# The opening of a hybrid Fourier/Hyena and attention block: loads, filters, modulation and norm in an order written out by hand

## The chip, the cores and the metric

The kernel runs on one core of one Trainium2 chip. The metric is the device time of one execution in microseconds (us). Work in a core is done by engines that run side by side, each with its own list of instructions: PE (matrix products), DVE (VectorE), ACT (ScalarE), POOL (GpSimd) and SP, which here issues the transfers from memory (DMA). An instruction waits on semaphores for what it needs from another engine.

## The reference

The block has two layers over 512 tokens and 256 context tokens of width 1024, in float32. Layer 0 has the mixer with which this case deals; layer 1 has latent attention; each layer ends in a gated feed-forward network (FFN) with a short convolution. Cut to the opening of layer 0:

```python
mod = silu(cond) @ w_mod + b_mod            # six parts: shift, scale, gate, twice
h = rms_norm(x) * (1 + scale) + shift       # for x and for the context
proj = h @ w_in                             # 1024 -> 4*128 (Fourier) + 3*512 (Hyena)
y_f = fft2(proj[..., :512]).real            # in four groups of 128
x0, x1, v = split(dwconv3(proj[..., 512:]), 3)

h_ = sin(f * (z @ w1 + b1)); h_ = sin(f * (h_ @ w2 + b2)); h_ = sin(f * (h_ @ w3 + b3))
h_ = (h_ @ w4) * decay                      # a filter in time, forward and backward halves
two_sided = concat(h_fwd, 0, reversed h_bwd)
spectrum = rfft(two_sided / sum(abs(two_sided)))
y_h = x0 * (irfft(rfft(v * x1) * spectrum) + v * x1 * bias)
out = concat(y_f, y_h) @ w_out
```

The filter and its spectrum are needed twice: for length 512 and for the context's length 256.

## The kernel before

**Precision.** Every product that counts is made of three matmuls: an operand is split into a high part (`hi`, L97, on ACT) and a low part (`lo`, L102, on DVE), and `mm3` (L116 to L118) adds high x high, high x low and low x high. A table or weight tile of 128 x 1024 (name `wr`) is loaded by SP (`wload`) and split in the same way into `wh` and `wl`; the normalized input has the parts `hh` and `hl`.

**The opening.** It has these parts, and the tile framework's scheduler orders the instructions of each engine from the order in the source, what depends on what, and its estimates of costs.

- The filter MLP (`filter_mlp`, `sine`): three rounds of a matmul (L330), eight DVE operations (L305 to L314) and a sine on ACT (L315).
- The time filters (`filter_time`), in six tiles of 128 positions: tiles 4 and 5 for the context, 0 to 3 for x. For each: two matmuls for 128 x 1024 results (L345), two products with the decay on DVE (L351, L352), their sum and difference on POOL (L357), which are split into high and low parts (`aph`, `apl`, `amh`, `aml`), two absolute values on ACT and their sum on POOL (L366). The sums of all tiles go through PE (L371) and a reciprocal on DVE (L373), which gives S.
- The spectra (`filter_spec`): two for the context and four for x, each a table times the filter tiles, then scaled with S (L403 to L405); `brow` is the bias in all partitions, which L381 rescales for each length; the Nyquist row comes from L389 to L392.
- The modulation: `gemv_pe` makes the shift and the scale of the first norm, in four chunks of 2 MB (`wm`): 16 matmuls with a 32-column operand, a copy on ACT (L182), small matmuls (L185) and an add on DVE (L190). The other parts come later and in pieces of 128 rows (`gemv_dve`), with a DVE product of the weight tile and the activated condition `sb` (L200). `make_A` turns scale and norm weight into the factor A.
- The norm (`norm`), for x (512 columns) and context (256): `stat` squares on ACT (L223) and sums on PE (L224); `fin` copies (L228), brings the sums into columns (`rt`, L232), takes 1/sqrt by Newton steps on DVE (`rsqrt`), and spreads it over the partitions (R, L238); `apply` multiplies on DVE (L248), adds the shift on ACT (L250, which gives `hh`) and takes the rest on DVE (L251, `hl`). There are eight tiles for x and eight for the context, so 32 DVE operations.

**The projections.** Sixteen tiles of w_in, 48 matmuls each, in the order 12, 8, 13, 9, 14, 10, 15, 11 (pairs v and x1), 4, 5, 6, 7 (x0), 0 to 3 (Uf). A projection of the Hyena part is convolved on the way out of PSUM (L294 on ACT, L295 and L296 on DVE); of a pair, POOL multiplies (L489, L490), DVE folds the halves (L494, L495), and PE transposes the result (`turn`, L501). The source puts a turn behind the next projection:

```python
hconv(12 + i, cv)
if folded:
    turn(i - 1, folded.pop())
hconv(8 + i, cx)
folded.append(fold(i, cv, cx))
...
hconv(4, x0[0])
turn(3, folded.pop())
```

A projection also issues one `gemv_dve`. The 32 tiles of layer 0's rest are spread over the 16 projections and, two per step, over the last steps of W_out (`res_proj` with `hook`); those of layer 1 go three to each step of the first FFN (`fill`).

Of the kernel before, what the change touches and what calls it, by code (L numbers as in the profile page):

```python
# [18 lines left out]
P = 128  # L19
D = 1024  # L20
KD = 8
# [29 lines left out]
class Builder:  # L51
# [10 lines left out]
    def pool(self, name, bufs=1, space=None, side=None):  # L62
        st = ExitStack()
        kw = {}
        if space is not None:
            kw["space"] = space
        if side is not None:
            kw["side"] = side
        p = st.enter_context(self.tc.tile_pool(name=name, bufs=bufs, **kw))
        self.stacks = getattr(self, "stacks", {})  # L70
        self.stacks[name] = st
        return p
# [31 lines left out]
    def wload(self, src, n=1024):  # L104

        raw = self.t(self.W, [P, 1024], F32, "wr")
        self.nc.sync.dma_start(raw[:, :n], src)
        h = self.t(self.W, [P, 1024], F32R, "wh")
        l = self.t(self.W, [P, 1024], F32R, "wl")
        self.hi(h[:, :n], raw[:, :n])  # L110
        self.lo(l[:, :n], raw[:, :n], h[:, :n])
        return h, l
# [57 lines left out]
    def gemv_pe(self, i, chunk):  # L170
# [3 lines left out]
        raw = self.t(self.wm, [P, 4096], F32, "wm")  # L174
        for half in range(2):
            nc.sync.dma_start(raw[:, 2048 * half : 2048 * half + 2048], self.I["wmod0a"][chunk, :, 2048 * half : 2048 * half + 2048])
# [34 lines left out]
    def norm(self, i, k, x, hh, hl, c0, n, tp):  # L211
# [33 lines left out]
        def apply(d):  # L245
            A, B = self.A[i][k][:, j, :], self.mod[i][:, 24 * k : 24 * k + 8, j]
            u = tp()
            nc.vector.scalar_tensor_tensor(u[:, :n], x[d][:, c0 : c0 + n], A[:, d : d + 1], box["R"][:, :n], op0=ALU.mult, op1=ALU.mult)  # L248
            dst = hh[d][:, c0 : c0 + n]
            nc.scalar.activation(dst, u[:, :n], AF.Identity, bias=B[:, d : d + 1])  # L250
            nc.vector.scalar_tensor_tensor(hl[d][:, c0 : c0 + n], u[:, :n], B[:, d : d + 1], dst.bitcast(F32), op0=ALU.add, op1=ALU.subtract)  # L251

# [64 lines left out]
    def filter_mlp(self):  # L317
        nc, I = self.nc, self.I
        p = self.pf
        zT = self.t(p, [66, 384], F32, "zT")  # L320
        fw = self.t(p, [P, 3, P], F32, "fw")
        w4 = self.t(p, [P, 1024], F32, "w4")
        nc.sync.dma_start(zT, I["zT"])
        nc.sync.dma_start(fw, I["fw"])
        nc.sync.dma_start(w4, I["w4"])
        h = zT
        for l in range(3):
            ps = self.ms()
            K = 66 if l == 0 else P
            nc.tensor.matmul(ps[:, :384], fw[:K, l, :], h[:K, :384], start=True, stop=True)  # L330
            h = self.t(self.S2, [P, 512], F32, "s2")
            self.sine(ps, self.col(f"fb{l + 1}"), h)
        return h, w4

    def filter_time(self, h3, w4, tts, nhalf):

        nc, I = self.nc, self.I
        v = nc.vector
        sums = []
        ap, am = [], []  # L340
        for i, tt in enumerate(tts):
            ps = self.mm()
            r0, c = 64 * (tt // 3), 128 * (tt % 3)
            for q in range(2):
                nc.tensor.matmul(ps[:, 512 * q : 512 * q + 512], h3[r0 : r0 + 64, c : c + 128], w4[r0 : r0 + 64, 512 * q : 512 * q + 512],  # L345
                                 start=True, stop=True)
            dec = self.t(self.S2, [P, 512], F32, "s2")
            nc.sync.dma_start(dec, I["decay"][tt])
            f = self.t(self.S2, [P, 512], F32, "s2")
            b = self.t(self.S2, [P, 512], F32, "s2")  # L350
            v.tensor_tensor(f, ps[:, 0:512], dec, op=ALU.mult)  # L351
            v.tensor_tensor(b, ps[:, 512:1024], dec, op=ALU.mult)  # L352
            if i == 0:
                v.memset(b[0:1, :], 0.0)
            for lst, op in ((ap, ALU.add), (am, ALU.subtract)):
                s = self.t(self.S2, [P, 512], F32, "s2")
                nc.gpsimd.tensor_tensor(s, f, b, op=op)  # L357
                tg = "ap" if lst is ap else "am"
                hi = self.t(p_ := self.pf, [P, 512], F32R, tg + "h", 4)
                lo = self.t(p_, [P, 512], F32R, tg + "l", 4)  # L360
                self.hi(hi, s)
                self.lo(lo, s, hi)
                lst.append((hi, lo))
            nc.scalar.activation(f, f, AF.Abs)
            nc.scalar.activation(b, b, AF.Abs)
            nc.gpsimd.tensor_tensor(f, f, b, op=ALU.add)  # L366
            sums.append(f)
        ps = self.ms()
        on = self.onesN[nhalf]
        for i, f in enumerate(sums):  # L370
            nc.tensor.matmul(ps, on, f, start=i == 0, stop=i == len(sums) - 1)  # L371
        S = self.t(self.pf, [P, 512], F32, "S")
        v.reciprocal(S, ps)  # L373
        return ap, am, S

    def filter_spec(self, ap, am, S, nhalf, fts, tt0):

        nc, I = self.nc, self.I
        v = nc.vector
        B = self.brow  # L380
        nc.vector.tensor_scalar(B, B, self.bscale / nhalf, None, op0=ALU.mult)  # L381
        self.bscale = nhalf
        nt = len(ap)
        ny = None
        if 0 in fts:
            ps = self.ms()
            for i in range(nt):
                for q in range(2):
                    nc.tensor.matmul(ps[0:1, :], self.altr, ap[i][q], start=i == 0 and q == 0, stop=i == nt - 1 and q == 1)  # L389
            ny = self.t(self.S2, [P, 512], F32, "s2")  # L390
            v.tensor_tensor(ny[0:1, :], ps[0:1, :], S[0:1, :], op=ALU.mult)
            v.tensor_tensor(ny[0:1, :], ny[0:1, :], B[0:1, :], op=ALU.add)  # L392
        H = []
        for ft in fts:
            th, tl = self.wload(I["ftab"][ft, :, 0 : 256 * nt], 256 * nt)
            ps = self.mm()
            for c, a in ((0, ap), (1, am)):
                for i in range(nt):
                    w = slice(256 * i + 128 * c, 256 * i + 128 * c + 128)
                    self.mm3(ps[:, 512 * c : 512 * c + 512], th[:, w], tl[:, w], a[i][0], a[i][1], i == 0, i == nt - 1)  # L400
            hr = self.t(self.S2, [P, 512], F32, "s2")
            hi = self.t(self.S2, [P, 512], F32, "s2")
            v.tensor_tensor(hr, ps[:, 0:512], S, op=ALU.mult)  # L403
            nc.gpsimd.tensor_tensor(hr, hr, B, op=ALU.add)
            v.tensor_tensor(hi, ps[:, 512:1024], S, op=ALU.mult)  # L405
            H.append((hr, hi))
        return H, ny


    def mixer(self):  # L410
# [13 lines left out]
        h3, w4 = self.filter_mlp()  # L424
        self.bscale = 1.0
        self.brow = self.t(self.pf, [P, 512], F32, "brow")
        nc.sync.dma_start(self.brow, I["hyb"].partition_broadcast(P))
        x = [self.t(xp, [P, TW], F32, f"x{d}") for d in range(KD)]
        self.gemv_pe(0, 0)
        apc, amc, Sc = self.filter_time(h3, w4, (4, 5), 256.0)  # L430
        self.gemv_pe(0, 1)
        for d in range(KD):
            nc.sync.dma_start(x[d][:, 0:512], I["xT"][d])
        Hc, nyc = self.filter_spec(apc, amc, Sc, 256.0, (0, 1), 4)
        ap, am, S = self.filter_time(h3, w4, (0, 1, 2, 3), 512.0)
        self.gemv_pe(0, 2)
        hh, hl = [], []
        n1, n2 = self.norm(0, 0, x, hh, hl, 0, T, tp), self.norm(0, 0, x, hh, hl, C0, C, tp)
        for d in range(KD):
            nc.sync.dma_start(x[d][:, C0 : C0 + C], I["cxT"][d])  # L440
        for d in range(KD):
            n1[0](d)
        n1[1](True)
        self.gemv_pe(0, 3)
        for d in range(KD):
            n2[0](d)
        n2[1](True)
        self.close("wm")
        hp = self.pool("hp", side="right")
        hh += [self.t(hp, [P, TW], F32R, f"hh{d}") for d in range(KD)]  # L450
        hl += [self.t(hp, [P, TW], F32R, f"hl{d}") for d in range(KD)]
        self.zero_pads(hh + hl)
        self.make_A(0, 0)
        H, ny = self.filter_spec(ap, am, S, 512.0, (0, 1), 0)
        for d in range(KD):
            n1[2](d)
            n2[2](d)
        H += self.filter_spec(ap, am, S, 512.0, (2, 3), 0)[0]
# [14 lines left out]
        def proj(m):  # L473
# [6 lines left out]
            self.gemv_dve(*gl.pop(0))  # L480
# [25 lines left out]

        folded = []
# [8 lines left out]
        hconv(4, x0[0])  # L516
        turn(3, folded.pop())
        for i in range(1, 4):
            hconv(4 + i, x0[i])
        for g in range(4):  # L520
# [227 lines left out]
    def layer0(self):  # L748
# [21 lines left out]
        def hook(stage, m):  # L770
            for _ in range(2):
                if gl:
# [11 lines left out]
        gl1 = [(1, jt, (0, 1) if jt < 16 else (0,)) for jt in range(48)]  # L784
# [512 lines left out]
```

## Time and profile before

| | |
|---|---|
| median of three runs | 1850.3 us (1850.04 to 1851.7) |
| the profiled execution: its own time | 1850.64 us |
| its span | 1848.8 us |
| busy: PE / DVE / ACT / POOL | 1724.1 / 1017.5 / 615.5 / 116.5 us |
| mean granted clock of PE | 0.951 |
| PE busy, 0 to 50, 50 to 100, 100 to 145 us | 30.78, 39.96, 34.88 us |
| DVE busy in the same | 21.91, 32.61, 33.31 us |
| DMA: moved, mean | 172.83 MB, 93 GB/s |

In the rows of the timeline the first number is the start in us from the beginning of the span, the second the duration; then come engine, line, operation, result and operands, sizes, and in brackets how long the engine had been idle and which instruction ended that. In the groups, the part after the bar is the total busy time in us, the mean of one in ns, and the idle time just before the group's instructions with what ended it. The rows of 40 digits are equal slices of the span or window: busy tenths, or for PEclk the clock that PE was granted in tenths of full speed.

### The profile page before, as it was taken

The page shows a single profiled execution, that of the slowest core. Times are in us where ns is not written, and L with a number is a line of the kernel's source. Part 1 is how long each engine was busy: PE and PEld are TensorE (multiplying, and loading weights), DVE is VectorE, ACT ScalarE, POOL GpSimd, SP SyncE. Part 2 cuts the span into 40 slices and gives each one's busy share as a digit, 9 for nine tenths or more (in the row PEclk, how much of TensorE's full clock was granted, in tenths as well). Part 3 has the DMA queues.
Part 4 walks back from the last instruction along what each step waited for, and adds up shares of the span by engine and source line. Part 5 has one row for each costly group of instructions (what it writes and reads, how often), then busy time and mean ns, then how long its engine had stood idle before and what let it go on. Part 6 is the DMA issues. An engine that isn't in the chain of part 4 may idle for free.

```text
span 1848.8 us, 21707 instructions
## 1 busy us (share of the span) xinstructions
PE 1724.1 (93%) x8742; PEld 1337.8 (72%) x8742; DVE 1017.5 (55%) x1669; ACT 615.5 (33%) x832; POOL 116.5 (6%) x194
## 2 busy tenths in 40 slices
PE   5779996799899999999999797899998999999999
PEld 1358885787688888888888575555554778888887
DVE  4669735887896435533233544666674554434433
ACT  2332222323322212221122334665663433233231
POOL 1401103310000000000000000110110000000000
PEclk8889996899999999999999978899998999999999
DMA  9213321254355224422112210000001322322222
GB/s 352 74 58 126 114 83 34 104 195 148 114 173 179 82 103 148 148 81 80 57 51 94 93 51 34 1 12 12 12 12 57 125 69 91 106 99 92 103 74 97
DMA packets 53249, 172.83 MB, mean 93 GB/s; under 512 B 6043, under 2 KB 8925, under 8 KB 52125
## 3 DMA queue, kind: packets, MB, share of 16 engines
q1 hardware_dynamic: 53149, 171.45, 27.0%
q8 instruction: 69, 1.13, 0.3%
q14 instruction: 31, 0.25, 0.0%
HBM read 167.23 MB, written 4.19 MB: 93 GB/s over the span
## 4 chain that ended last, share of the span: by engine, by line
PE 79%; DVE 10%; ACT 4%; POOL 3%; DMA 2%; issue 2%; SPq 0%; POOLq 0%; ACTq 0%; DVEq 0%
PE mm L116 22%; PE mm L117 21%; PE mm L118 21%; PE pv L1034 2%; PE z L1022 2%; PE ms L224 2%; DVE wl L102 1%; DVE S L1012 1%; PE s L116 1%; PE s L988 1%; DVE junk L200 1%; PE s L117 1%; DMA wm<-wmod0a 1%; PE s L118 1%; DVE hl L251 1%
## 5 line engine op out<-in xcount | busy, mean ns | idle before, releaser
L116 PE MATMUL mm<-hh,wh 128*128 128x512 f32 (+3 forms) x1376 | 487.0, 357 | 7.1 <-ACT hh L250 7.0
L117 PE MATMUL mm<-hl,wh 128*128 128x512 f32 (+3 forms) x1376 | 486.6, 354 | 2.8 <-DVE hl L251 2.5
L118 PE MATMUL mm<-hh,wl 128*128 128x512 f32 (+3 forms) x1376 | 486.0, 354 | 1.3 <-DVE wl L102 1.3
L97 ACT ACTIVATE wh<-wr 128x1024 fp32r<-128x1024 f32 (+2 forms) x202 | 208.0, 1030 | 725.6 <-PE mm L117 676.5
L102 DVE TENSOR_TENSOR wl<-wr,wh 128x1024 fp32r<-128x1024 f32 (+2 forms) x202 | 244.3, 1210 | 315.8 <-ACT wh L97 308.1
L116 PEld LDWEIGHTS mm<-hh,wh 128*128 128x128 f32 (+1 forms) x1376 | 261.1, 191 | 56.6 <-issue 10.4
L117 PEld LDWEIGHTS mm<-hl,wh 128*128 128x128 f32 (+1 forms) x1376 | 261.3, 190 | 43.2 <-DVE hl L251 5.6
L118 PEld LDWEIGHTS mm<-hh,wl 128*128 128x128 f32 (+1 forms) x1376 | 260.9, 190 | 39.4 <-DVE wl L102 2.1
L116 PE MATMUL mm<-ah,wh 128*128 128x512 f32 (+1 forms) x528 | 187.9, 356 | 0.0
L117 PE MATMUL mm<-al,wh 128*128 128x512 f32 (+1 forms) x528 | 187.6, 356 | 0.0
L118 PE MATMUL mm<-ah,wl 128*128 128x512 f32 (+1 forms) x528 | 187.3, 355 | 0.0
L200 DVE SCALAR_TENSOR_TENSOR junk<-wr,sb 128x1024 bf16<-128x1024 f32 x128 | 157.7, 1232 | 30.3 <-DMA wr<-wmodT 30.0
L684 DVE SCALAR_TENSOR_TENSOR xr<-mm,mod,xr 128x512 f32<-128x512 f32 (+1 forms) x100 | 62.2, 642 | 198.8 <-PE mm L118 198.5
L116 PEld LDWEIGHTS mm<-ah,wh 128*128 128x128 f32 x528 | 99.1, 188 | 19.3 <-DVE xr L684 2.5
L117 PEld LDWEIGHTS mm<-al,wh 128*128 128x128 f32 x528 | 99.2, 188 | 15.3 <-issue 0.8
L118 PEld LDWEIGHTS mm<-ah,wl 128*128 128x128 f32 x528 | 99.1, 188 | 14.5
L1003 ACT ACTIVATE S<-s,rks 128x512 f32<-128x512 f32 x96 | 63.4, 688 | 44.0 <-PE s L118 43.0
L1012 DVE TENSOR_TENSOR S<-S,mb 128x1536 f32<-128x1536 f32 x32 | 54.8, 1752 | 20.7 <-POOL mb L1009 20.7
L721 ACT ACTIVATE fg<-fg 128x772 f32<-128x772 f32 (+1 forms) x44 | 32.6, 741 | 99.6 <-DVE fg L296 88.9
L1034 PE MATMUL pv<-S,V 128*64 128x512 f32 x192 | 59.1, 622 | 0.0
L1022 PE MATMUL z<-S,ones 128*32 128x512 f32 x192 | 42.5, 696 | 13.3 <-ACT S L1013 10.9
L1013 ACT ACTIVATE S<-S 128x1536 f32<-128x1536 f32 x32 | 47.1, 1482 | 17.9 <-DVE S L1012 17.8
(299 smaller groups left out, 2253.0 us busy)
## 6 DMA issues: line engine op xcount, KB each, us to landing
wr<-w_up SPq DMA_DIRECT2D x88, 512.0 KB, 3.3
wr<-wmodT SPq DMA_DIRECT2D x80, 512.0 KB, 3.3
wr<-w_dn SPq DMA_DIRECT2D x32, 512.0 KB, 3.2
wm<-wmod0a SPq DMA_DIRECT2D x8, 1024.0 KB, 8.8
wr<-w_in SPq DMA_DIRECT2D x16, 512.0 KB, 3.2
wr<-w_dn SPq DMA_DIRECT2D x20, 384.0 KB, 3.0
wr<-w_out SPq DMA_DIRECT2D x12, 512.0 KB, 4.1
wr<-w_o SPq DMA_DIRECT2D x12, 512.0 KB, 3.3
```

The source lines that it names most:

```text
L97: self.nc.scalar.activation(dst, src, AF.Copy)
L102: (eng or self.nc.vector).tensor_tensor(dst, src, hi.bitcast(F32), op=ALU.subtract)
L116: mmul(out, wh, xh, start=start, stop=False)
L117: mmul(out, wh, xl, start=False, stop=False)
L118: mmul(out, wl, xh, start=False, stop=stop)
L200: nc.vector.scalar_tensor_tensor(junk, raw, 1.0, self.sb[:, j, :], op0=ALU.mult, op1=ALU.mult, accum_out=acc)
L684: nc.vector.scalar_tensor_tensor(x[m][:, a2:b2], ps[:, a2:b2], mod[:, 8 * sec + m, j : j + 1], x[m][:, a2:b2], op0=ALU.mult, op1=ALU.add)
L1003: nc.scalar.activation(S[j // 3][:, j % 3, :], ps, AF.Copy, scale=rs[:, 2 * j + a : 2 * j + a + 1])
L1012: v.tensor_tensor(s, s, mb3.to_broadcast([P, 3, T]), op=ALU.subtract)
L1013: nc.scalar.activation(s, s, AF.Exp)
L1022: nc.tensor.matmul(z[32 * g : 32 * g + 32, :], self.ones32, Ss[g // 2][(2 * k + g % 2) // 3][:, (2 * k + g % 2) % 3, :], start=k == 0, sto ...
L1034: nc.tensor.matmul(pv[64 * a : 64 * a + 64, :], V[:, k, 64 * h : 64 * h + 64], Ss[a][k // 3][:, k % 3, :], start=k == 0, stop=k == 5, tile ...
```

## The change

The opening of `mixer` is written out in one order, and the scheduler keeps that order on PE, DVE and SP; ACT and POOL are still ordered by it. The functions of the filter are cut into steps for that (`filter_mm`, `filter_pm`, `filter_lo`, `filter_sum`, `filter_spec`, `filter_scale`, `filter_nyquist`, `gemv_raw`, `wraw`, `wsplit`); what they compute is the same, with one rescaling of `brow` less. `apply` can be called in two steps, high part and low part. The apply steps of the norm come ahead of the filter spectra 1 to 3 of x. Three other things change with it: every pool gets `reuse_waits="tile"`, so that a tile that takes over memory waits for the tiles that had it and not for the whole pool; the projections come in the order 0, 1, 4 to 7, then the pairs, turn 3, then 2 and 3; and eight `gemv_dve` tiles of layer 0 move from W_out to the first steps of the first FFN. In the changed file the lines stand some 8 to 110 further down: the sine is L334, `gemv_pe`'s matmuls and add L189 and L200, `filter_mm` L361, the turn L607.

```diff
+        kw["reuse_waits"] = "tile"
         p = st.enter_context(self.tc.tile_pool(name=name, bufs=bufs, **kw))
...
-        h3, w4 = self.filter_mlp()
+        with self.tc.manual_schedule(engines={ENG.PE, ENG.DVE, ENG.SP}):
+            layer = self.filter_mlp()
+            for d in range(KD):
+                nc.sync.dma_start(x[d][:, 0:512], I["xT"][d])
...
+            decays(4, 5)
+            wm = [self.gemv_raw(0)]
+            decays(0, 1)
+            for d in range(KD):
+                nc.sync.dma_start(x[d][:, C0 : C0 + C], I["cxT"][d])
+            wm.append(self.gemv_raw(1))
+            decays(2, 3)
+            nc.sync.dma_start(self.brow, I["hyb"].partition_broadcast(P))
+            tc_ = [self.wraw(I["ftab"][ft, :, 0:512], 512) for ft in range(2)]
+            wm.append(self.gemv_raw(2))
+            tx = [self.wraw(I["ftab"][0])]
+            h = layer(1, layer(0, None))
+            for d in range(KD):
+                s1(d)
+            h3 = layer(2, h)
+            f1(True)
+            pc = [self.filter_mm(h3, 4), self.filter_mm(h3, 5)]
+            self.gemv_pe(0, 0, wm[0])
+            wm.append(self.gemv_raw(3))
+            pmc = [self.filter_pm(pc[i], dec[4 + i], i == 0) for i in range(2)]
+            px = [self.filter_mm(h3, 0)]
+            for d in range(KD):
+                s2(d)
+            ac = [self.filter_lo(pm) for pm, _ in pmc]
+            Sc = self.filter_sum([f for _, f in pmc], 256.0)
+            pmx = [self.filter_pm(px[0], dec[0], True)]
+            px.append(self.filter_mm(h3, 1))
+            pmx.append(self.filter_pm(px[1], dec[1], False))
+            f2(True)
+            self.gemv_pe(0, 1, wm[1])
+            ax = [self.filter_lo(pm) for pm, _ in pmx]
+            self.filter_skip(256.0)
+            twc = [self.wsplit(r, 512) for r in tc_]
+            Hc = []
+            for ft in range(2):
+                ps = self.filter_spec(ac, twc[ft])
+                Hc.append(self.filter_scale(ps, Sc))
+                px.append(self.filter_mm(h3, 2 + ft))
+            nyc = self.filter_nyquist(ac, Sc)
+            for i in (2, 3):
+                pmx.append(self.filter_pm(px[i], dec[i], False))
+            self.gemv_pe(0, 2, wm[2])
+            twx = [self.wsplit(tx[0])]
+            ax += [self.filter_lo(pm) for pm, _ in pmx[2:]]
+            S = self.filter_sum([f for _, f in pmx], 512.0)
+            self.filter_skip(512.0)
+            psx = self.filter_spec(ax, twx[0])
+            self.gemv_pe(0, 3, wm[3])
+            self.make_A(0, 0)
...
+            twx.append(self.wload(I["ftab"][1]))
+            both(0, 0)
+            H = [self.filter_scale(psx, S)]
+            both(1, 0)
+            both(0, 1)
+            psx = self.filter_spec(ax, twx[1])
...
+            both(7, 0)
+            both(6, 1)
+            last = both(7, 1)
+            H.append(self.filter_scale(psx, S))
+            H.append(self.filter_scale(self.filter_spec(ax, twx[3]), S))
...
-            self.gemv_dve(*gl.pop(0))
+            if m < 3:
+                with self.tc.issue_after(last.ins):
+                    self.gemv_dve(*gl.pop(0))
+            else:
+                self.gemv_dve(*gl.pop(0))
...
+        for g in range(2):
+            nc.scalar.copy(Uf[g], proj(g)[:, :TW])
+        for i in range(4):
+            hconv(4 + i, x0[i])
         folded = []
...
-        hconv(4, x0[0])
         turn(3, folded.pop())
-        for i in range(1, 4):
-            hconv(4 + i, x0[i])
-        for g in range(4):
+        for g in range(2, 4):
             nc.scalar.copy(Uf[g], proj(g)[:, :TW])
...
-                if gl:
+                if len(gl) > 8:
                     self.gemv_dve(*gl.pop(0))
...
-        gl1 = [(1, jt, (0, 1) if jt < 16 else (0,)) for jt in range(48)]
+        gl1 = gl + [(1, jt, (0, 1) if jt < 16 else (0,)) for jt in range(48)]
```

## What I expected before it ran

> **What bounds the kernel now.** I read the slices of the span first, then the costliest groups, then the timeline of the opening, engine by engine. Two rows of the slices, then three rows of the groups:
>
> ```profile
> PE   5779996799899999999999797899998999999999
> PEclk8889996899999999999999978899998999999999
> ...
> L116 PE MATMUL mm<-hh,wh 128*128 128x512 f32 (+3 forms) x1376 | 487.0, 357 | 7.1 <-ACT hh L250 7.0
> L117 PE MATMUL mm<-hl,wh 128*128 128x512 f32 (+3 forms) x1376 | 486.6, 354 | 2.8 <-DVE hl L251 2.5
> L118 PE MATMUL mm<-hh,wl 128*128 128x512 f32 (+3 forms) x1376 | 486.0, 354 | 1.3 <-DVE wl L102 1.3
> ```
>
> PE is full except in the first three slices (46 us each) and near slices 7 and 23. So the change can pay only in the opening, and there the time that counts is when the 16 projections (L116 to L118, operands hh, hl, wl) can run through. The 7.0 and 2.5 us of waits for hh and hl are what "h made ahead" is after. The end of the projections and the opening's start:
>
> ```profile
> 268.00 0.78 ACT L521 COPY x<-mm 128x772 f32<-128x772 f32 x1
> ...
> 276.45 0.79 ACT L521 COPY x<-mm 128x772 f32<-128x772 f32 x1
> ```
>
> One projection takes 276.45 - 268.00 = 8.45 us, and one with a turn (the transposes of L501) 1.29 more. Going back from the last read, 276.45 - 16 x 8.45 - 4 x 1.29 = **136.1 us** is when a row of projections without stalls would have begun. PE began the first at 129.21, so stalls cost 6.9. I price the change by this one number.
>
> ```profile
> 25.08 0.52 ACT L315 ACTIVATE s<-s 128x384 f32<-128x384 f32 x1 [5.42 <-DVE s L314]
> ...
> 26.65 0.63 ACT L97 ACTIVATE wh<-wr 128x512 fp32r<-128x512 f32 x1 [0.57 <-DMA wr<-ftab]
> ```
>
> The filter MLP's last sine ends at 25.60, after three rounds of 5.93 us. The first table split follows it on ACT, and waits there for its table.
>
> **The change, part by part.** Of the same instructions one brow scale (L381, 0.42 us on DVE) is gone, with nothing waiting for it: 0. The order on PE, DVE and SP is now written out; ACT and POOL keep the scheduler's. In the compiled order ACT runs: sine 0, split of context table 0, of table 1, sine 1, 8 squares of x, split of table 0, two silus of sb, sine 2. An engine runs its list in order, so two sines stand behind loads. Queued behind them are the 8 squares, and PE's layer 2, statistics and all filters.
>
> When do these loads land? SP's new order puts x, wm 0 and 1, cx, five decays and brow ahead of the context tables (10.78 MB up to the second of them) and sb at 14.45 MB. The loads of before, in slices of 1.5 us:
>
> ```profile
> GB/s 0 170 229 285 130 246 401 431 431 431 426 414 389 406 388 385 402 419 422 419 373 361 258 307 399 415 423 399 426 410 265 0 11 0 0 0 0 0 0 5
> ...
> sb<-cboth SPq DMA_DIRECT2D x1, 512.0 KB, 8.3
> ```
>
> Summed, 10.8 MB are in at 31.5 us and 14.5 MB at some 42. The slow slices of the 1-KB rows of cx (258, 307) now come earlier, so I take 33.5 (31 to 37) and 43. Then: sine 1 ends 34.65; 8 squares of 0.53 (L223), 38.9; their last matmul 39.4; layer 2 (1.62) 41.05; its DVE part (3.63) 44.7; ACT has ended sb's silus (1.04 each, L167) at 45.0; **sine 2 ends 45.5, not 25.6: 20 us late.**
>
> From here each link waits for the one before, because the new order puts the norm and the modulation of one gemv ahead of the next filter part on the same queue:
> - 45.5 to 58.6: stat copy 0.59, rt 0.95, 12 rsqrt steps 2.35, R 1.16, four cold passes of filter_mm at 0.85, gemv 0 2.7 (between 1.9 warm and 3.3 cold), its copy 0.58, L185 and the add with their gaps 1.2. DVE's add for gemv 0 stands ahead of the first filter products, which are therefore late too.
> - 58.6 to 76.0: products 1.7, four POOL operations (L357, 1.3 each) to 65.8, ACT's last of that tile to 67.6, 8 squares of cx to 70.2 (they stand behind these on ACT), statistics and sum to 72.6, reciprocal 3.36. Before, this reciprocal began at 48.77 and ended at 52.1.
> - 76.0 to 98.0: products 1.7, POOL to 83, ACT to 85, copy, rt, rsqrt 88.2, R 89.4, gemv 1 and its add to 94.3, four low parts 2.7, brow and table split 1.0.
> - 98.0 to 121.2: context spectrum 0 (cold) 102.3, spectrum 1, filter_mm and Nyquist 108.8, products 112.5, POOL 116.5, ACT 118.3, gemv 2's copy and L185 119.9, table split 121.2.
> - to 133.6: four low parts and sum 123.4, spectrum 0 129.6, gemv 3 131.5, its add and make_A 133.6. Only now has DVE the factors A and the shift.
>
> On SP the load of wm 3 waits for gemv 0 on PE (56.7), and the one of table 1 behind it for the context table's split on DVE (97): with 3.3 us to land it is there by 102 and needed at 130, so 0; it would cost from 28 us later on.
>
> DVE then has, ahead of the low part of w_in 0 that projection 0's third matmul needs (row 135 of its list): 32 apply operations, which before took 17.95 us (122.02 to 142.55, other work taken out), four pairs of scales 4.8, the Nyquist pair 1.3, four splits 4.7: 28.7, so **162.3**. Before, half of these ran under a spectrum; now the three spectra run under them, and PE is the one that waits. PE starts the row cold:
>
> ```profile
> 113.78 1.19 PE L238 MATMUL ms<-cst,rq_r 128*128 128x128 f32 x4 [5.06 <-DVE rq_r L134]
> ...
> 126.24 0.57 PE L116 MATMUL mm<-amh,wh 128*128 128x512 f32 x1
> ...
> 126.65 0.39 PE L117 MATMUL mm<-aml,wh 128*128 128x512 f32 x1
> ```
>
> After 5.06 us of idle time a matmul took 0.63 until 126.24, later 0.39 (pitch 0.43 and 0.23). From the restart at 120.95 that is 5.3 us at half rate, 2.7 lost; the restart at 37.74 was through by 42, 2.2 lost, which I take (work without gaps, as here): 164.5, so **+28.4** on 136.1. The Trainium skill ("TensorE: Matmul & The Clock Gate", Part 1: The HAM clock gate) has full rate after one busy window of about 3.4 us; an estimate by it is 1.7 lost for each restart, and with two restarts the sum would be 1 us lower. The trace shows the longer stretch, so it decides.
>
> Next, the projections: now Uf 0, Uf 1, x0 (4 to 7), then the pairs 12/8 to 15/11, turn 3, Uf 2, Uf 3. Before, projection 4 ran between pair 3 and its turn; now turn 3 follows projection 11 at once on PE. The chain of a pair:
>
> ```profile
> 171.26 0.98 ACT L294 ACTIVATE tm<-mm,pcol 128x772 f32<-128x772 f32 x1
> ...
> 175.76 2.21 POOL L489 TENSOR_TENSOR tm<-tm,tm 128x512 f32<-128x512 f32 x1 [15.30 <-DVE tm L296]
> ...
> 179.09 0.98 PE L501 MATMUL mm<-cst,tm 128*128 128x128 f32 x6 [0.31 <-DVE tm L494]
> ```
>
> That is 7.8 us with two gemv rows of 1.22 inside; the cover was the 8.45 of the next projection. With the cover gone PE idles some 7.0 and restarts cold (2.3): **+9.3** (7 to 10).
>
> Smaller parts. Waits per tile at pool reuse: those of before are mostly on work long done; PE's waits that could go are those for oh in the attention, 2.2 us in all; I take -0.5, bounds 0 and -2.2. Eight gemv tiles (16 rows of 1.22 on DVE) move from W_out's late half to the first FFN ups: from 450 to 490 PE is idle 5.4 us, of which wl has 1.3; in 490 to 600 PE is full with DVE at 85 of 110 us busy, and the total of the fills grows from 48 to 56 tiles, which 19 of 22 ups hold. I take -0.7, bounds +1 and -5. The gemv rows of the first three projections (L200) come behind the last hl: 0, as no projection waits for them.
>
> Sum: 28.4 + 9.3 - 0.5 - 0.7 = +36.5 on the profiled execution's 1850.64 (span 1848.8 and 1.8 around it) = 1887.1; the median of the runs, 1850.3, stands 0.3 below it: **1886.8 us**.
>
> **Rivals.**
> - The chain is longer still (0.14): POOL at its mean beside DVE (1.54, not 1.3) over some 12 serial operations is 3, loads at their late end 3.5, a colder PE 2 to 4, so 1895 to 1904. For it: each link has one owner and no slack. Against: some links are rounded up.
> - Turn 3 is covered after all, or the idle time is short (0.12): 1.0 in place of 9.3, 1878. Against: the compiled order of PE has one projection between turns 2 and 3, and none behind it.
> - The loads do not gate the sines (0.08): h3 at 25.6 and the chain 20 us earlier, lag 8.4, so 1867. Against: the order on ACT, and 14.45 MB at the shown rate. The Trainium skill ("Perfetto Trace Analysis", Per-instruction lifecycle) calls ACT's, DVE's and GPSIMD's queues strict FIFO; the waits of the 26.65 row agree.
> - Other side, faster (0.06): the parts interleave. If norm and gemv hide under the filters instead of following them, only DVE's work is the bound. Before it was busy 78 us of the first 130, to which 12.5 of apply work up to 142.55 and some 15 of waits in the MLP (25.6 less 3 x 3.63) come: h at 105 to 110. That gains 26 to 31, less the turn's 9.3, and with the 1.2 saved it is 18 to 23: some 1830. The point: projection 0's third matmul must come before about 126 us (136.1 - 9.3 + 1.2, less 2.2 for a cold PE). For it: h then waits for no spectrum. Against: make_A waits for gemv 3 at 131, behind three spectra in PE's list, by rows with no slack for 30 us.
> - The change does nothing that can be measured (0.02): gain and turn cancel, 1850.
>
> **How the numbers follow.** The forecast has 0.58. Its own range is 1876 to 1896: loads 2.5 early to 3.5 late, turn 7 to 10, DVE's tail 24 to 31, clock, small parts. 8 in 10 leave out the faster and equal cases (0.08) and most of the far end: 1863, under the load rival with the small gains, to 1904. A measurement of this kernel tells about 0.2% (3.7 us) from no change; faster by over that 0.06, within 0.02, slower 0.92.
>
> **What would show it.** In the changed profile: ACT's second sine near 34 and the third near 45, both behind a DMA wait; DVE idle until gemv 0's add (line 200 of the changed kernel) near 58; make_A near 133; projection 0's third matmul near 162, waiting for wl; the last Uf read near 314; 7 us of PE idle ahead of the last six transposes; granted clock under 0.8 for most of 50 to 160. I am wrong if the third sine ends before 32, if make_A comes before 110, or if the projections start before 130.

## The result, and the profile after

The changed kernel takes 1893.8 us in the median (1892.0 to 1895.6), 1.0233 times the kernel before, with an interval of 1.0215 to 1.0251: 43 us slower. The profiled execution has a span of 1892.0 (1848.8 before). The slices of the page, and the three groups with the operands hh, hl and wl, of which the projections are a part:

```profile
PE   2568998689999999999999979899998999999999
PEclk9578999689999999999999987799999999999999
...
L123 PE MATMUL mm<-hh,wh 128*128 128x512 f32 (+3 forms) x1376 | 487.4, 357 | 11.6 <-ACT hh L259 6.1
L124 PE MATMUL mm<-hl,wh 128*128 128x512 f32 (+3 forms) x1376 | 486.9, 355 | 1.2 <-DVE hl L263 0.7
L125 PE MATMUL mm<-hh,wl 128*128 128x512 f32 (+3 forms) x1376 | 485.8, 354 | 2.3 <-DVE wl L103 2.3
```

PE did the same work (1724.8 us busy); the first four slices are emptier, and in the second the granted clock is half. The timeline of ACT shows where it begins:

```profile
32.92 1.28 ACT L98 ACTIVATE wh<-wr 128x512 fp32r<-128x512 f32 x2 [21.07 <-DMA wr<-ftab]
34.12 0.51 ACT L334 ACTIVATE s<-s 128x384 f32<-128x384 f32 x1
...
45.20 0.52 ACT L334 ACTIVATE s<-s 128x384 f32<-128x384 f32 x1 [1.76 <-DVE s L333]
```

ACT stood 21 us in front of a table that only the context spectra need, from 104 on. Sines 1 and 2 end at 34.6 and 45.7. The timeline of PE in the next link, and the windows row of 50 to 100 us (busy us of PE, PEld, DVE, ACT and POOL, then the granted clock):

```profile
52.62 7.19 PE L361 MATMUL mm<-w,s 64*128 64x512 f32 x8
59.74 3.64 PE L189 MATMUL ms<-wm,sT 128*32 128x512 f32 x16
64.14 1.87 PE L195 MATMUL ms<-cst,s 128*128 128x2 f32 x8 [0.76 <-ACT s L192]
```

```profile
50.00:100.00 50.00, 29.33 (x84) 13.11 (x87) 17.14 (x31) 13.34 (x28) 16.51 (x12) 0.57 0.11 42
```

The three rows stand in series, all at half rate, while DVE and ACT wait: DVE worked 17 of 50 us, and gemv 0's add, the end of the first link, ended a wait of 15.6:

```profile
66.04 0.17 DVE L200 TENSOR_TENSOR mod<-ms,pcol 128x8 f32<-128x8 f32 x1 [15.55 <-PE ms L195]
```

Then the end of the chain on DVE (make_A, the low part of w_in 0), the turn on PE, and the last read of a Uf on ACT:

```profile
146.94 0.24 DVE L218 SCALAR_TENSOR_TENSOR A<-mod,pcol 128x8 f32<-128x8 f32 x2
...
174.21 1.20 DVE L103 TENSOR_TENSOR wl<-wr,wh 128x1024 fp32r<-128x1024 f32 x1
```

```profile
305.94 1.51 PE L607 MATMUL mm<-cst,tm 128*128 128x128 f32 x6 [6.73 <-DVE tm L600]
```

```profile
326.45 0.78 ACT L628 COPY x<-mm 128x772 f32<-128x772 f32 x1
```

The last read was at 276.45 before: **50.0 us later**. The rest of the kernel is 6.8 us shorter (1892.0 - 326.45 = 1565.55, against 1572.35), which makes the 43.2 of the spans.

### The profile page after: what moved, and what is told of

Its sections match the earlier page's. It is cut to its first block, busy times and chain, and to the rows that moved or that the text cites. A ratio compares the mean times of both kernels' runs of the same rounds, so it can differ in the third digit from the quotient of the medians.

```text
span 1892.0 us, 21712 instructions
## 1 busy us (share of the span) xinstructions
PE 1724.8 (91%) x8742; PEld 1342.9 (71%) x8742; DVE 1016.3 (54%) x1668; ACT 615.2 (33%) x832; POOL 126.1 (7%) x194
## 4 chain that ended last, share of the span: by engine, by line
PE 79%; DVE 11%; ACT 4%; POOL 3%; issue 2%; DMA 1%; SPq 0%; POOLq 0%; DVEq 0%; ACTq 0%
PE mm L123 21%; PE mm L124 21%; PE mm L125 21%; PE pv L1141 2%; PE ms L234 2%; PE z L1129 2%; DVE wl L103 1%; DVE S L1119 1%; DVE hl L263 1%; PE s L1095 1%; PE s L123 1%; PE s L124 1%; PE s L125 1%; ACT S L1110 1%; DVE nt L258 1%
## 5 line engine op out<-in xcount | busy, mean ns | idle before, releaser
L1120 ACT ACTIVATE S<-S 128x1536 f32<-128x1536 f32 x32 | 47.1, 1482 | 17.9 <-DVE S L1119 17.9
```

Source lines behind the costliest of these rows:

```text
L1120: nc.scalar.activation(s, s, AF.Exp)
```

## The experiments

Ratios are to the kernel before, measured in the same session. "Last read" is the one of the row above, in the profile.

**1. Which load holds the sines.** Two edits on the changed kernel:

```diff
-        with self.tc.manual_schedule(engines={ENG.PE, ENG.DVE, ENG.SP}):
+        with self.tc.manual_schedule(engines={ENG.PE, ENG.DVE, ENG.SP, ENG.Activation}):
```

and, in the second run, also:

```diff
             tx = [self.wraw(I["ftab"][0])]
+            self.load_sb()              # now only the two loads
...
+            self.silu_sb()              # the two silus
             twx = [self.wsplit(tx[0])]
...
         self.close("pf")
-        self.load_sb()
```

> The changed kernel, with ACT kept in the hand order too: the three table splits no longer stand ahead of sines 1 and 2, but the two silus of sb (loaded behind 14.45 MB) still stand ahead of sine 2. Theory (two loads gate the sines, and the later one decides): sine 1 ends near 18 in place of 34.6, sine 2 still waits for sb and ends near 44 in place of 45.7, so the time falls by about 2 us, to some 1892. Rival (the first wait alone made the delay): sine 2 ends near 29 and the time falls by 16 to 17, to some 1877.

> As the run before, and the silus of sb come behind gemv 2's copy, so that no load of a table or of sb stands ahead of a sine. Theory (the chain behind the third sine has no slack): sine 2 ends near 28.5 in place of 45.7 (x lands near 12, layer 2 follows the statistics of x), the rest keeps its length, and the time falls by about 17, to 1876 to 1878. Rival (other loads or the cold clock take it back, since wm 1 and the tables land at 28 to 40): less than half of that, 1885 or more.

Measured: 1.0233 (1.0216 to 1.0251) and 1.0151 (1.0136 to 1.0167). ACT of the first run:

```profile
16.41 0.52 ACT L334 ACTIVATE s<-s 128x384 f32<-128x384 f32 x1 [5.41 <-DVE s L333]
...
41.21 1.06 ACT L174 ACTIVATE sb<-sb 128x1024 f32<-128x1024 f32 x1 [20.10 <-DMA sb<-cboth]
...
43.42 0.51 ACT L334 ACTIVATE s<-s 128x384 f32<-128x384 f32 x1
```

Sine 1 came 18 us earlier and nothing came of it: the same wait of 20 us moved to sb's silu. With both loads out of the way sine 2 comes 18 us earlier than in the changed kernel:

```profile
26.99 0.52 ACT L336 ACTIVATE s<-s 128x384 f32<-128x384 f32 x1 [5.94 <-DVE s L335]
```

The last read is at 308.30, 18.2 us earlier. The theory held for the chain; the two waits are one behind the other, and only the later counts. That the time fell by 15 and not by 18 (0.0082 of 1851) lies behind the last read, of which more under 3. The first run's 2 us were not seen in the time either, though its last read is 0.6 earlier.

**2. The turn.**

```diff
+        nc.scalar.copy(Uf[2], proj(2)[:, :TW])
         turn(3, folded.pop())
-        for g in range(2, 4):
-            nc.scalar.copy(Uf[g], proj(g)[:, :TW])
+        nc.scalar.copy(Uf[3], proj(3)[:, :TW])
```

> The changed kernel, with projection 2 moved ahead of turn 3, so that it covers the fold of the last pair. Theory: PE's 6.7 us of idle time before the last six transposes goes, with the cold stretch behind it, 8.2 in all: 1885 to 1886. Rival (the wait only moves, to the first context spectrum, which needs the last turn's parts): less than 3 us, above 1890.

Measured: 1.0198 (1.0183 to 1.0214), which is 6.5 us less than the changed kernel's ratio. The transposes wait for nothing now:

```profile
306.58 0.82 PE L607 MATMUL mm<-cst,tm 128*128 128x128 f32 x6
```

The last read is at 316.75, 9.7 us earlier (0.9 of that is from the opening). So the 8.2 us at this place are gone, and 0.6 more; the stretch behind it was longer than in the changed kernel's profile, so the time shows less.

**3. The waits per tile alone**, on the kernel before:

```diff
+        kw["reuse_waits"] = "tile"
         p = st.enter_context(self.tc.tile_pool(name=name, bufs=bufs, **kw))
```

> The kernel before with one line more: every pool waits per tile. In the changed kernel the stretch behind the opening was 6.8 us shorter than before, 2.4 of it in the spectral part and the inverse, 3.6 around the output product of the attention, where PE waited 1.3 in place of 2.2 us for oh and its clock did not fall. Theory (the waits per tile made that): 1844 to 1846. Rival (the order of the projections and the moved gemv tiles made it, or chance in the clock): within 1.5 us of before, 1849 to 1851.5.

Measured: 0.9982 (0.9969 to 0.9994), 3.3 us, between the two: the theory held for the part at the attention's output product, and not for the other. PE there, first in the kernel before, then in this one:

```profile
1416.94 1.65 PE L116 MATMUL mm<-oh,wh 128*128 128x512 f32 x3 [2.18 <-ACT oh L97]
```

```profile
1417.75 0.97 PE L117 MATMUL mm<-oh,wh 128*128 128x512 f32 x3 [1.26 <-ACT oh L98]
```

This kernel is 1.7 us behind at that place (last read 278.13), and the wait is 0.9 shorter; behind it PE's clock had not fallen (three matmuls in 0.97 us, not 1.65), and from here to the second FFN's first activation 80.6 us pass in place of 83.3. In all ten other profiles with the waits per tile this wait is 1.26 too, and the three matmuls take 0.96 or 0.97. The other stretch, from the last read to the first activation of the first FFN, took 222.3 before, 222.4 here, 222.2 in both runs of experiment 1, but 219.3 in the changed kernel's profile. The code from there on is the same in the changed kernel and in experiment 1, so these 3 us are neither the waits nor the moved gemv tiles, of which no gain is seen there. In the 35 us behind the last read the granted clock was 0.75 in the changed kernel's profile, and 0.65, 0.65 and 0.69 in those of before, of this kernel and of the first of experiment 1. The two kernels with extra matmuls in experiment 4, which have the same code there, took 219.5 and 219.6, at 0.80 and 0.81. So with the same code the shorter stretch comes with the higher clock; the kernel of experiment 2, whose order just ahead is another, took 223.6 at 0.73. What set the clock there was not tried and stays open.

**4. The order of a link, and the clock.** Both on the second kernel of experiment 1. First the filter products ahead of gemv 0:

```diff
-            self.gemv_pe(0, 0, wm[0])
-            wm.append(self.gemv_raw(3))
             pmc = [self.filter_pm(pc[i], dec[4 + i], i == 0) for i in range(2)]
+            self.gemv_pe(0, 0, wm[0])
+            wm.append(self.gemv_raw(3))
```

> The kernel of the run without loads ahead of the sines (ACT in hand order, sb late; 1.0151 of before), with one link of the chain turned round: the context's filter products come ahead of gemv 0 on PE and DVE. Theory (gemv 0's 3.64 us on PE, 0.6 of copy and 1.9 up to DVE's add stand in the chain between the filter matmuls and the products): the products start 5 us earlier and the time falls by about 5, to 1.0125 of before. Rival (another wait, that of POOL or of the cold clock, is late anyway): within 1.5 us of that kernel.

Measured: 1.0111 (1.0096 to 1.0126), last read 304.08, 4.2 earlier. The theory held in sign and, by the last read, in size; the ratio fell by more (7.4 us), but the two intervals allow 4 as well.

Then extra matmuls ahead of the waits, in two sizes:

```diff
+    def warm(self, ps, n):
+        for _ in range(n):
+            self.nc.tensor.matmul(ps[:, 0:512], self.onesN[512.0], self.w4[:, 0:512], start=True, stop=True)
...
-            f1(True)
+            f1(True, (6, 4))       # ahead of rt and of R; second size (4, 2)
...
-                s2(d)
+                s2(d, 14)          # ahead of the context's statistics; 7
-            f2(True)
+            f2(True, (16, 4))      # (8, 2)
-            self.gemv_pe(0, 2, wm[2])
+            self.gemv_pe(0, 2, wm[2], 14)    # ahead of its small matmuls; 7
```

> The same kernel without loads ahead of the sines, with 58 more matmuls of 128 x 512 (two passes each) that write into tiles which the real ones overwrite, ahead of the waits for the norms' columns and R, the context's statistics and gemv 2's small matmuls, so that PE does not sit idle there. They are no part of the computation. Theory (the clock, at 0.60 in 27 to 80 us and 0.8 to 130, makes the chain longer: filter matmuls 7.19 in place of 3.8, gemv 0 3.64 in place of 1.9, statistics and sum 6.5 in place of 3.6, and so on, some 16 in all): the time falls by 10 to 16, to 1.007 to 1.010 of before. Rival (the waits on DVE, ACT and POOL set the pace, PE's part is hidden): it falls by less than 4, or rises by the dummies' own time.

Measured: 1.0145 (1.0128 to 1.0162), last read 315.92: the expectation failed, because I had sized the sets as if a matmul took one pass, and each of these makes two, which stand in the trace as two matmuls. A set of 16 took 15.7 us, where PE's whole wait without it was 10.4. So once more with half:

> As the run with the extra matmuls (1.0145 of before), with 30 of them in place of 58: a set now takes no longer than the wait that it fills (a matmul of two passes takes 0.98 us, so 8 of them for the 7.5 us before the context's columns, where 16 took 15.7 and were late themselves). Nothing else differs; they are no part of the computation. In the run before, gemv 0's add came 4.0 us earlier than without extra matmuls, and then their own length took that back. Theory (the cold clock lengthens the chain): the last Uf read comes 8 to 13 us earlier than the 308.3 of the kernel without extra matmuls, and the time is 1.008 to 1.011 of before. Rival (PE's part of the chain is hidden but for gemv 0): 2 to 5 us, 1.0125 to 1.014.

Measured: 1.0084 (1.0062 to 1.0105), last read 297.57, **10.7 us earlier** than without. The windows row of 50 to 80 us, without and with:

```profile
50.00:80.00 30.00, 10.30 (x32) 5.16 (x32) 13.72 (x22) 11.83 (x25) 15.43 (x12) 0.61 0.06 24
```

```profile
50.00:80.00 30.00, 23.73 (x83) 10.49 (x83) 12.87 (x27) 9.32 (x22) 9.12 (x8) 0.89 0.02 4
```

PE is busy more than twice as long there, in good part with the extra matmuls, at 0.89 of the clock in place of 0.61, and the chain is shorter: the eight filter matmuls of the first link take 3.70 us in place of 7.19, gemv 0 takes 1.92 in place of 3.64, and its add comes at 40.39 in place of 46.73. The cold clock was a term of its own.

**5. The other way round: projections first.** What the runs say is that the chain is long because links that need each other stand in line with nothing beside them. Projections 0, 1, 2 and 4 to 7 write into x tiles and need nothing of the filters, so they can be what lies beside. In its last form the order is:

```python
wm = [self.gemv_raw(0), self.gemv_raw(1)]     # then cx, wm 2, decays 4 and 5, w_in 0
h = layer(1, layer(0, None))
...                                           # statistics of x
f1(True, 0)                                   # norm of x up to 1/sqrt
self.gemv_pe(0, 0, wm[0])
f1(True, 1)                                   # R
h3 = layer(2, h)
self.gemv_pe(0, 1, wm[1])
...                                           # statistics of the context
self.gemv_pe(0, 2, wm[2])
f2(True, 0)
self.gemv_pe(0, 3, wm[3])
f2(True, 1)
pc = [self.filter_mm(h3, 4), self.filter_mm(h3, 5)]
self.make_A(0, 0)
...                                           # 32 apply operations
ps = pmm(wt)                                  # projection 0
wt = self.wload(I["w_in"][1])
nc.scalar.copy(Uf[0], ps[:, :TW])
...                                           # products of 4, 5, 0; projection 1; ...
```

The first form had the filter products of tiles 4, 5 and 0 between the gemv chunks; the second had `nc.scalar.copy(Uf[g], ...)` behind the filter tiles, and the products of tiles 0 and 1 behind the reciprocal.

> Another order in full, from what the runs so far point to: the norm and the four gemv chunks first (their loads first, too), then the 32 apply operations, then projections 0, 1, 2 and 4 to 7 with the filter's steps and spectra between them, each table and weight split one step ahead; the pairs; projection 3 as the cover of turn 3; ACT in hand order, waits per tile. Theory (the chain's links cost what they do because nothing lies beside them; behind projections they are covered): projection 0 is through near 75 us, the row of projections needs 135 + 5 and the filter's matmuls between them 45 at a warm clock, so the last read of a Uf comes near 240 to 250 in place of 276.45, and the time is 1815 to 1825. Rival (DVE, with splits, scales and convolutions in one queue, stalls PE in each step): no better than before, 1850 or more.

Measured: 0.9994 (0.9979 to 1.001), last read 278.29. The expectation failed: make_A came at 80.4, and projection 0 was through at 99 and not near 75. On ACT the copies for the context's norm (56.6) and for gemv 3 (77.7) stood behind filter tiles that waited for POOL, an order on ACT that holds up the chain, as in the changed kernel.

> The order with projections first, mended: in its first form (0.9994 of before) the filter products and their ACT work stood between the gemv chunks, so that make_A came at about 80 us, and the first projection was through at 99. Now the four gemv chunks and the two norms come first on all four queues, filter matmuls of the context behind them, and every other filter step behind the apply operations. Theory (what stands ahead of make_A in the queues of ACT and DVE sets the start): make_A near 50, projection 0 through near 70, last Uf read near 245, 1815 to 1820 (0.980 to 0.983 of before). Rival (PE stalls in the projections in the same measure as make_A comes earlier, because DVE and POOL carry the filters there): the last Uf read stays above 265, and the time within 0.99 to 1.0.

Measured: 0.9946 (0.9928 to 0.9965), last read 269.14. make_A (48.9) and projection 0 (through at 71) came as expected, the sum did not. PE's waits in the projections:

```profile
79.81 0.80 PE L123 MATMUL mm<-hh,wh 128*128 128x512 f32 x1 [4.36 <-ACT x L541]
97.78 0.77 PE L123 MATMUL mm<-hh,wh 128*128 128x512 f32 x1 [5.01 <-DVE s L376]
120.19 3.77 PE L366 MATMUL mm<-w,s 64*128 64x512 f32 x4 [3.18 <-DVE s L444]
```

The first operand of a projection was there; what the first two rows waited for is their accumulator, which a copy on ACT and a product on DVE had not yet read. The third row, filter matmuls, waited in the same way for a scale on DVE.

> The order with projections first, mended once more (0.9946 of before in its second form; make_A at 48.9 and projection 0 through at 71 there, as expected, but PE then idled 4.4, 5.0 and 3.2 us, with cold stretches behind: projection 1 waited for the accumulator that ACT's copy of Uf 0 held, since this copy stood behind the filter tiles on ACT, projection 2 for the one that the products of tiles 0 and 1 held, since these stood behind a reciprocal on DVE). Now the copies stand ahead of the filter tiles on ACT, and the products ahead of the reciprocal and the low parts on DVE. Theory (these places in the queues are what the waits come from): the three waits go, 12 to 18 us with their cold stretches, last Uf read 251 to 257, time 0.985 to 0.988 of before, 1823 to 1830. Rival (DVE is the bound there, and the waits move to its other steps): less than 5 us, 0.992 or more.

Measured: **0.9869 (0.985 to 0.9889)**, 1827.3 us against 1852.4 beside it: faster than both kernels. The last read:

```profile
253.74 0.78 ACT L659 COPY x<-mm 128x772 f32<-128x772 f32 x1
```

That is 15.4 earlier than in the second form, from places in the queues alone: the copies on ACT, the products on DVE, and the context's Nyquist row, which moved behind the filter matmuls of tiles 2 and 3 as well. What each is worth was not tried. Some 4.5 us of wait for a table split are left at 101, and the whole is far from the 240 that I had first set.

## Why the prediction was right, point by point

The sign, the cause and the place were right: ACT's order put two sines behind loads, each link waited for the one before, turn 3 lost its cover. The time came out 7 us above the forecast and inside its own range. That hides two errors that partly cancel: the last read came 12.3 us later than forecast (50.0 and not 37.7 behind the kernel before), and the stretch behind it was 5.6 us shorter. Without the second the time would have been some 1899, outside the range, so that it lies inside is in part luck.

- **Sine 2** at 45.7, forecast 45.5: right. Worth 18 us (experiment 1), where I said 20 late.
- **45.5 to 58.6**, the first link, took to 66.0: the mis-sized term. The filter matmuls of two tiles are eight, not four (7.19 us, forecast 3.4): the kernel before has 24 for its six tiles, and I had counted those of one. The columns (rt) took 1.87 and R 2.05, forecast 0.95 and 1.16; gemv 0 took 3.64 (2.7), its small matmuls 1.87 where they take 1.05 with a warm clock. From there each link was a little longer again: reciprocal through at 85.6 (76.0), gemv 1's add 104.2 (94.3), gemv 2's 132.0 (some 120), make_A 146.9 (133.6). Beside the filter matmuls, gemv 0 and a context spectrum, I had put the cold clock only as one term of 2.2 at the end; it lay on the whole chain, and experiment 4 gives 10.7 for it.
- **DVE's tail**, forecast 28.7: 28.5 from make_A to the end of w_in 0's low part (146.9 to 175.4). Right, so the row of projections began 13 us later than forecast, all of it from the chain above.
- **The turn**, forecast 9.3: 8.2, from the reads at 300.09 and 317.97 (17.9 us, where a step with a turn takes 9.7). POOL's product took 1.26 and not 2.21, with no gemv rows in the way; PE's idle time was 6.7.
- **Waits per tile**, forecast -0.5 with a bound of -2.2: -3.7 in experiment 3's profile, outside the bound (0.9 up to the first matmul of the W_o stage, 2.7 from there to the second FFN). I bounded it by the wait of 2.2 for oh, and left out that a shorter wait may spare a cold stretch.
- **The moved gemv tiles**, forecast -0.7: no gain is seen. Up to the first FFN's first activation both runs of experiment 1 take 222.2 us with them moved, against 222.3 and 222.4 without; from there to the second FFN's it is 997.7 in the changed kernel and 997.8 in experiment 3.
- Sum behind the last read: -6.8 in the profile, forecast -1.2; 3.7 are the waits per tile, and 3 go with a higher clock behind the last read, whose cause is open (experiment 3): nothing in the prediction stood for them.

With the parts taken one by one, of the 50 us at the last read 18.2 are the loads ahead of the sines, 10.7 the cold clock, 8.2 the turn and 4.2 the place of gemv 0. The remaining 9 are not tried; by the rows above they are the other links in line. The parts come from different kernels, and that they add up was not tried either.

The rivals: the longer chain (1895 to 1904) had the direction in which the chain missed, and a colder PE among its reasons; only the shorter stretch behind the last read kept the time below it. That the loads don't gate was wrong, and in experiment 1 the kernel without them came to 1879, not 1867, since the chain behind them was longer than I had it. The Trainium skill ("Perfetto Trace Analysis", Per-instruction lifecycle) calls ACT's queue strictly first in, first out; the 20.10 us of ACT behind sb's load, with sine 2's operand ready at 27.2, agree. The rival on the other side had a real mechanism, but for another order: experiment 5 is 25 us faster than before, by parts that lie beside each other.

## What to carry to other kernels

When an order is written by hand, read each queue for what stands behind a load or behind another engine's slow chain; a wait that is taken away counts only if none stands behind it (experiment 1), and a few places in the queues were worth 15 us together (experiment 5). Long chains of small steps pay twice, because PE's clock falls while it waits (0.61 here, and 0.89 with the waits filled, in experiment 4). Put work that needs nothing beside the chain: that, and not a tighter chain, made the faster kernel.

## What the runs showed of the hardware that I had not expected

- **PE stayed at half rate while it was busy.** In the changed kernel it ran from 50.64 to 63.4 without a gap, most of it filter matmuls on 64 rows, at a granted clock of 0.50, and the next four filter matmuls, behind 0.8 us of waiting and the small matmuls of gemv 0, were still slow. In the second kernel of experiment 1 the same sequence, from 32.13 to 44.9, was slow too (0.50), and the four behind it fast. The four, in this order:

```profile
65.94 3.78 PE L361 MATMUL mm<-w,s 64*128 64x512 f32 x4
```

```profile
46.62 1.98 PE L363 MATMUL mm<-w,s 64*128 64x512 f32 x4
```

The statistics of x from 17.46 there, 4.90 us, had the clock up at the next matmuls (layer 2, two in 0.91). The Trainium skill ("TensorE: Matmul & The Clock Gate", Part 1: The HAM clock gate) has full rate after some 3.4 us of sustained work; the statistics agree, the filter matmuls don't (over 10 us). Whether the 64 rows are the cause was not tried.
- **POOL beside DVE.** Three scalings that take 1.3 each alone, as at 142.38 in the kernel before, took 18 us together beside DVE's work: the first 12.2, over most of DVE's apply operations, the second 1.3 and the third 4.6.

```profile
160.86 17.97 POOL L438 TENSOR_TENSOR s<-s,brow 128x512 f32<-128x512 f32 x3 [9.52 <-DVE s L437]
```

Here nothing waited for them; the profile's spans of POOL are rough, so the size is to be taken with care.
